# How the sample tokens' values reach all partitions: a DRAM buffer in place of selection matmuls

## The chip, the core and the metric

The kernel runs on one core of a Trainium2 chip. The metric is the device time in microseconds of one execution. Five engines run side by side, each with an instruction queue of its own that is worked off in order: TensorE (PE; its weight loads are shown apart as PEld), VectorE (DVE), ScalarE (ACT), GpSimd (POOL) and SyncE (SP). POOL and SP are used here mostly to issue DMAs; a DMA that must wait for something holds up what stands behind it on the queue of the engine that issues it.

## The reference, cut to what matters

The whole is one inference step of two decoder layers for 256 prompt tokens and 8 sample tokens (one token of each of 8 requests). Layer 0 attends over a window, layer 1 is a gated linear recurrence (HGRN2) with 12 heads, each with a state matrix of 128 x 128 for every request. The change concerns the recurrence for the 8 sample tokens:

```python
q, f, iv, mq, g = _split(jnp.einsum('btd,de->bte', h, w_in), HG_SPLITS)
fg = lb + (1.0 - lb) * jax.nn.sigmoid(f)
qh, kh, vh = jax.nn.silu(q), 1.0 - fg, iv
# one token: o and the new state
o = (q . k) v + (q * fg) @ state
state = fg[..., None] * state + k[:, None] * v[None, :]
```

(The last two lines write out what the chunked form of the reference comes to for one token.) The new state of every request and head is an output, 8 x 12 x 128 x 128 numbers in f32. All inputs and outputs are f32.

## The kernel before

**Layout.** Features lie on partitions, tokens along a row: 256 prompt and 8 sample tokens (T = 264). A product in near-f32 accuracy is made of f16 halves: each weight block of 128 x 2048 is loaded as f32 (`raw`), ScalarE writes the high half (line 92), VectorE the rest (line 93), and TensorE makes three passes (lines 297 to 299). One projection is 48 matmuls of 264 columns.

**The stream.** `Stream` walks over a list of units, each a weight block or a piece of cache or state with a function that uses it. Four `raw` buffers and four split buffers `hl` are in turn; loads are issued by SP (line 77) as buffers come free. A state block (one head's state, 8 requests x 128 x 128; added in lines 1154 to 1157) is split too, but its f32 form is held until its unit is done, since the new state is written into it and stored from it.

**Layer 1, per pair of heads.** Units run in the order f, f, v, v, q, state, (g), q, state, (g); g only for the first eight heads (four pairs). After each pair a side job `hg_side` does the recurrence of the prompt in pieces between the projections that follow. The order in which each engine takes its instructions is set when the program is built, by a scheduler that simulates the engines with assumed durations: what is written one after the other may be moved.

**The sample tokens' path.** `hv_unit` (line 930) projects v for one head and keeps it in f32 (`vt`) and, for the 8 sample columns, as f16 halves (`vs`). `hv_rows` (line 948) runs one unit later: it transposes the prompt part (line 952) and the halves (line 955, `hvr`), and VectorE copies the 16 rows to `vr` (line 956). `state_unit` (line 1106) then forms q times the forget gate (qf) and q times k (qk), multiplies the split state with qf (lines 1127, 1128: `hos`), sums qk over the partitions with an f32 matmul against constant weights (line 1130), and puts the output together (lines 1131 to 1133). For the new state every partition needs the row v of a request: a matmul with a selection matrix `sel` copies row b of `vr` to all 128 partitions in PSUM (line 1137, `vb`, four requests to a bank, eight matmuls a head). ScalarE scales the old state by the forget gate (line 1141), VectorE adds k times v (line 1142), and POOL stores the result (line 1145, `out_ss`).

**What stands near.** On POOL the store of the prompt's state (`out_sp`, line 1075). On VectorE the SiLU of q (line 728, `hqs`), on which the products `hd` (line 1030) and, over qa (line 1031) and qsp (line 987), the products `hs` on TensorE wait.

Of the kernel before, what the change touches and what calls it, by code (L numbers as in the profile page):

```python
# [32 lines left out]
SW = 1024.0  # L33
SA = 8.0
SP = 1024.0
SK = 2048.0
CP = 1.0 / (SW * SA)
# [92 lines left out]
def trunk_kernel(  # L130
# [17 lines left out]
    ident_d: bass.AP,  # L148
    onehot_d: bass.AP,
    mask_d: bass.AP,  # L150
    sel_d: bass.AP,
    y_o: bass.AP,
    mk_o: bass.AP,
    mv_o: bass.AP,
# [7 lines left out]
    nc = tc.nc  # L162
    mm = nc.tensor.matmul

    cp = ctx.enter_context(tc.tile_pool(name="cp", bufs=1))
# [3 lines left out]
    def bank(tag, bufs, name):  # L169
        return ps.tile([P, 512], F32, tag=tag, name=name, bufs=bufs)  # L170
# [21 lines left out]
    nc.gpsimd.memset(nones, -1.0 / P)  # L192
    ones_rms = cp.tile([P, P], F32, name="ones_rms")
    nc.vector.memset(ones_rms, 1.0 / 128.0)
    eps_rms = cp.tile([P, 1], F32, name="eps_rms")
    nc.vector.memset(eps_rms, RMS_EPS)

# [49 lines left out]
    def split_from(dst_hi, dst_lo, src, scale):  # L247
        split_all([(dst_hi, dst_lo, src)], scale)
# [631 lines left out]
    def open_l1():  # L880
        l0.close()
        p1 = l1.enter_context(tc.tile_pool(name="p1", bufs=1))
        H["p"] = p1
        H["mask"] = p1.tile([P, NMASK], I32, name="mask_t")
        nc.gpsimd.dma_start(H["mask"], mask_d)
        H["sel"] = p1.tile([2 * TS, TS, P], F16, name="sel_t")
        nc.gpsimd.dma_start(H["sel"], sel_d)
        H["ksp"] = [p1.tile([P, 2, 2, TP], F16, name=f"ksp{i}") for i in range(4)]
        for t in H["ksp"]:
            nc.gpsimd.memset(t, 0.0)  # L890

    def f_unit(h):
        def fn(hl):
            if h == 0:
                drain()
                open_l1()
            p1 = H["p"]
            pt = proj(hl, xhl, T, f"f{h}")
            i = h % 2
            if i == 0:  # L900
                cur["fg"] = p1.tile([P, 2, T], F32, tag="fg", name=f"fg{h}", bufs=2)
                cur["kk"] = p1.tile([P, 2, T], F32, tag="kk", name=f"kk{h}", bufs=2)
                cur["ks8"] = p1.tile([P, 2, TS], F32, tag="ks8", name=f"ks8{h}", bufs=2)
            fg, kk, ks8 = cur["fg"][:, i], cur["kk"][:, i], cur["ks8"][:, i]
            th = p1.tile([P, T], F32, tag="th", name=f"th{h}", bufs=2)
            nc.scalar.activation(th, pt, AF.Tanh, scale=0.5 * CP)
            half, mid, half_k, nhalf_k = (hl_lb[:, k, h : h + 1] for k in range(4))
            nc.scalar.activation(fg, th, AF.Identity, bias=mid, scale=half)
            nc.scalar.activation(kk, th, AF.Identity, bias=half_k, scale=nhalf_k)
            nc.vector.tensor_scalar_mul(ks8, kk[:, TP:T], 1.0 / (SA * SK))  # L910

        return fn

# [11 lines left out]

        return fn

    later, due = [], []

    def hv_unit(h):  # L930
        def fn(hl):
            p1 = H["p"]
            i = h % 2
            pt = proj(hl, xhl, T, f"hv{h}")
            if i == 0:
                cur["vn"] = p1.tile([P, 2, 2, P], F32, tag="vn", name=f"vn{h}", bufs=2)
                cur["vr"] = p1.tile([2 * TS, 2, P], F16, tag="vr", name=f"vr{h}", bufs=2)
                cur["vt"] = p1.tile([P, 2, T], F32, tag="vt", name=f"hvt{h}", bufs=1)
            vt = cur["vt"][:, i]
            vs = p1.tile([P, 2 * TS], F16, tag="vs", name=f"vs{h}", bufs=2)  # L940
            nc.scalar.activation(vt, pt, AF.Copy, scale=CP)
            split_from(vs[:, :TS], vs[:, TS:], pt[:, TP:T], 1.0 / SW)
            vn, vr = cur["vn"], cur["vr"]
            later.append(lambda: hv_rows(h, vt, vs, vn, vr))

        return fn

    def hv_rows(h, vt, vs, vn, vr):
        i = h % 2
        pt = bank("pt", 2, f"hvp{h}")  # L950
        for c in range(2):
            nc.tensor.transpose(pt[:, c * P : (c + 1) * P], vt[:, c * P : (c + 1) * P], ident)
        nc.scalar.activation(vn[:, i].rearrange("p c v -> p (c v)"), pt[:, :256], AF.Copy)
        p16 = ps.tile([2 * TS, P], F16, tag="pt", name=f"hvr{h}", bufs=2)
        nc.tensor.transpose(p16, vs, ident16)
        nc.vector.tensor_copy(vr[:, i], p16)

    def early_gate(j):
        def fn(hl):
# [146 lines left out]
    def state_unit(h):  # L1106
        def fn(hl):
            p1 = H["p"]
            pi, i = h // 2, h % 2
            raw = stream.raw[state_at[h]][:, : TS * P]  # L1110
            R = raw.rearrange("p (b v) -> p b v", b=TS)
            v = hl[:, :, : TS * P].rearrange("p s (b v) -> p s b v", b=TS)
            vr, fgs, ks8 = cur["vr"][:, i], cur["fg"][:, i, TP:T], cur["ks8"][:, i]
            qs, ks, vts = (cur[n][:, i, TP:T] for n in ("q", "kk", "vt"))
            if i == 0:
                osb[pi] = p1.tile([P, 2, T], F32, tag="osb", name=f"osb{pi}", bufs=2)
            qk = p1.tile([P, TS], F32, tag="qk", name=f"qk{h}", bufs=2)
            qf = p1.tile([P, TS], F32, tag="qf", name=f"qf{h}", bufs=2)
            qfh = p1.tile([P, TS, 2], F16, tag="qfh", name=f"qfh{h}", bufs=2)
            nc.vector.scalar_tensor_tensor(qf, qs, SA * 0.5 * CP, fgs, op0=ALU.mult, op1=ALU.mult)  # L1120
            nc.vector.scalar_tensor_tensor(qk, qs, P * 0.5 * CP / SK, ks, op0=ALU.mult, op1=ALU.mult)
            nc.scalar.activation(qfh[:, :, 0], qf, AF.Copy)
            nc.vector.tensor_tensor(qfh[:, :, 1], qf, qfh[:, :, 0], op=ALU.subtract)
            po = bank("ms", 1, f"hos{h}")
            pov = po[:, : 2 * TS].rearrange("p (b s) -> p b s", s=2)
            for b in range(TS):
                mm(pov[:, b], v[:, 0, b], qfh[:, b], start=True, stop=False)
                mm(pov[:, b, 0:1], v[:, 1, b], qfh[:, b, 0:1], start=False, stop=True)
            pq = po[:, 2 * TS : 3 * TS]
            mm(pq, ones_rms, qk, start=True, stop=True)  # L1130
            nc.vector.tensor_reduce(qf, pov, axis=AX.X, op=ALU.add)
            nc.vector.tensor_tensor(qk, pq, vts, op=ALU.mult)
            nc.vector.scalar_tensor_tensor(osb[pi][:, i, TP:T], qf, 1.0 / (SA * SA), qk, op0=ALU.mult, op1=ALU.add)
            for g in range(2):
                pvb = bank("pt", 2, f"vb{h}{g}")
                for bb in range(4):
                    mm(pvb[:, bb * P : (bb + 1) * P], H["sel"][:, 4 * g + bb], vr, start=True, stop=True)
# [77 lines left out]
def _constants():  # L1215
    c = {}
    c["ident"] = np.eye(P, dtype=np.float32)
    oh = np.zeros((33, 383 + P), np.float32)
    d = 255 - np.arange(383)
    ok = (d >= 0) & (d < 128)  # L1220
    oh[np.where(ok, _bucket(d), 32), np.arange(383)] = np.where(ok, 1.0 / CSWA, 1.0)
    slot = np.arange(P)
    oh[_bucket(np.where(slot == 0, 0, 128 - slot)), 383 + slot] = 1.0 / CSWA
    c["onehot"] = oh
    s = np.arange(P)
    m = np.zeros((P, NMASK), np.int32)
# [5 lines left out]
    sel = np.zeros((2 * TS, TS, P), np.float16)  # L1232
    for b in range(TS):
        sel[b, b] = 1
        sel[TS + b, b] = 1
    c["sel"] = sel
    return c


# [55 lines left out]
def unlayout(r):  # L1295
# [15 lines left out]

INS = [
    "xT", "memT", "w_kv", "w_in0", "w_in1", "w_mk", "w_mv", "w_o", "c_mk", "c_mv", "c_sk", "c_sv",
    "state", "small", "relb", "ident", "onehot", "mask", "sel",
]


# [18 lines left out]
```

## Time and profile before

| | |
|---|---|
| median of 3 runs | 912.54 us (911.29 to 913.2) |
| the profiled execution | 912.57 us, its span 910.8 us |
| mean granted TensorE clock | 0.995 |
| TensorE busy | 895.5 us (98%) |
| VectorE busy | 701.9 us (77%) |
| ScalarE busy | 577.0 us (63%) |
| moved by DMA | 198.41 MB, 218 GB/s over the span |

The span is the time from the first to the last instruction. A line such as "L1137 PE MATMUL vb<-vr,sel_t" names the line of the code, the engine, the operation, and the tile written and the tiles read. Start times are microseconds from the span's start. Matmuls overlap, so their durations add up to more than the time they take; what one costs is the distance from its start to the next one's. "<-" behind a waiting time names what ended it. A clock of 1.00 is full speed.

### The profile page before, as it was taken

How to read it: one execution, taken by the hardware profiler on the slowest of the kernel's cores; microseconds unless marked ns; L12 is line 12 of the kernel's file. 1: busy time of each engine (PE TensorE's matmuls, PEld its weight loads, DVE VectorE, ACT ScalarE, POOL GpSimd, SP SyncE). 2: the span in 40 equal slices, each digit the busy share in tenths (PEclk: the TensorE clock that was granted, in tenths of full speed). 3: DMA queues.
4: the chain of work that ended last, by engine and by line, in shares of the span. 5: the costliest groups of instructions: out<-in, count | busy, mean ns of one | idle time of the engine just before them, and what ended most of it. 6: DMA issues, size and time to landing. Idle time of an engine off the chain costs nothing.

```text
span 910.8 us, 21139 instructions
## 1 busy us (share of the span) xinstructions
PE 895.5 (98%) x8913; PEld 760.7 (84%) x8913; DVE 701.9 (77%) x1280; ACT 577.0 (63%) x980; POOL 34.6 (4%) x63
## 2 busy tenths in 40 slices
PE   9999999999999999999999999999999999899996
PEld 6888989678888888866888888888888888788885
DVE  6869877669886666696697897978789899767645
ACT  6757776567664543576766777676778676945323
POOL 1100010000000000002000000000000000000000
PEclk9999999999999999999999999999999999999998
DMA  9999566567685555555384555727454778566302
GB/s 345 383 335 330 189 244 217 194 210 259 257 320 189 204 208 187 191 203 195 127 308 146 196 183 185 282 100 268 150 212 165 264 270 318 186 226 230 141 1 96
DMA packets 36412, 198.41 MB, mean 218 GB/s; under 512 B 4572, under 2 KB 8445, under 8 KB 16093
## 3 DMA queue, kind: packets, MB, share of 16 engines
q1 hardware_dynamic: 31632, 181.55, 55.6%
q0 software_dynamic: 4640, 15.44, 4.6%
q8 instruction: 70, 1.15, 0.5%
q14 instruction: 26, 0.21, 0.1%
q10 hardware_dynamic: 44, 0.07, 0.0%
HBM read 179.80 MB, written 17.22 MB: 216 GB/s over the span
## 4 chain that ended last, share of the span: by engine, by line
PE 87%; ACT 5%; DVE 5%; DMA 2%; issue 1%; SPq 0%; ACTq 0%; DVEq 0%
PE o L297 6%; PE o L299 6%; PE o L298 6%; PE g L299 6%; PE g L297 6%; PE g L298 6%; PE q L297 2%; PE hv L298 2%; PE hv L297 2%; PE q L298 2%; PE q L299 2%; PE hv L299 2%; ACT hl L92 2%; PE f L299 2%; PE f L297 2%; PE f L298 2%
## 5 line engine op out<-in xcount | busy, mean ns | idle before, releaser
L93 DVE SCALAR_TENSOR_TENSOR hl<-raw,hl 128x2048 f16<-128x2048 f32 (+2 forms) x176 | 376.9, 2145 | 96.6 <-ACT hl L92 95.9
L92 ACT ACTIVATE hl<-raw 128x2048 f16<-128x2048 f32 (+2 forms) x176 | 314.2, 1790 | 118.1 <-PE o L299 73.9
L297 PEld LDWEIGHTS <-hl 128*128 128x128 f16 (+1 forms) x2176 | 209.9, 98 | 34.0 <-issue 2.9
L299 PEld LDWEIGHTS <-hl 128*128 128x128 f16 (+1 forms) x2176 | 209.9, 98 | 33.4 <-DVE hl L93 2.1
L298 PEld LDWEIGHTS <-hl 128*128 128x128 f16 (+1 forms) x2176 | 209.9, 98 | 32.1 <-issue 1.6
L299 PE MATMUL g<-xhl,hl 128*128 128x264 f16 x512 | 141.3, 276 | 1.5 <-DVE hl L93 1.5
L297 PE MATMUL g<-xhl,hl 128*128 128x264 f16 x512 | 141.5, 276 | 0.0
L298 PE MATMUL g<-xhl,hl 128*128 128x264 f16 x512 | 141.3, 276 | 0.0
L299 PE MATMUL o<-mix,hl 128*128 128x264 f16 x512 | 141.2, 276 | 0.0
L298 PE MATMUL o<-mix,hl 128*128 128x264 f16 x512 | 141.2, 276 | 0.0
L297 PE MATMUL o<-mix,hl 128*128 128x264 f16 x512 | 140.8, 276 | 0.3 <-DVE xres L742 0.3
L297 PE MATMUL q<-xhl,hl 128*128 128x264 f16 x192 | 53.0, 276 | 1.0 <-DVE kst L245 1.0
L297 PE MATMUL f<-xhl,hl 128*128 128x264 f16 x192 | 52.9, 276 | 0.4 <-DVE mvhl L245 0.4
L297 PE MATMUL hq<-xhl,hl 128*128 128x264 f16 x192 | 53.0, 276 | 0.0
L298 PE MATMUL hq<-xhl,hl 128*128 128x264 f16 x192 | 53.0, 276 | 0.0
L299 PE MATMUL hq<-xhl,hl 128*128 128x264 f16 x192 | 53.0, 276 | 0.0
L298 PE MATMUL hv<-xhl,hl 128*128 128x264 f16 x192 | 53.0, 276 | 0.0
L297 PE MATMUL hv<-xhl,hl 128*128 128x264 f16 x192 | 53.0, 276 | 0.0
L299 PE MATMUL hv<-xhl,hl 128*128 128x264 f16 x192 | 53.0, 276 | 0.0
L298 PE MATMUL q<-xhl,hl 128*128 128x264 f16 x192 | 53.0, 276 | 0.0
L299 PE MATMUL q<-xhl,hl 128*128 128x264 f16 x192 | 53.0, 276 | 0.0
L299 PE MATMUL f<-xhl,hl 128*128 128x264 f16 x192 | 52.9, 276 | 0.0
(311 smaller groups left out, 1625.4 us busy)
## 6 DMA issues: line engine op xcount, KB each, us to landing
raw<-in_w_in SPq DMA_DIRECT2D x88, 1024.0 KB, 5.8
raw<-in_w_o SPq DMA_DIRECT2D x32, 1024.0 KB, 4.9
raw<-in_w_mk SPq DMA_DIRECT2D x8, 1024.0 KB, 4.8
raw<-in_w_mv SPq DMA_DIRECT2D x8, 1024.0 KB, 5.1
raw<-in_c_mk SPq DMA_DIRECT2D x8, 1024.0 KB, 5.2
raw<-in_c_mv SPq DMA_DIRECT2D x8, 1024.0 KB, 4.9
raw<-in_state SPq DMA_DIRECT2D x12, 512.0 KB, 5.0
out_ss<-raw POOLq DMA_DIRECT2D x12, 512.0 KB, 2.9
```

What stands on the lines that cost most here:

```text
L92: hi = self.nc.scalar.activation(hl[:, 0, s], raw[:, s], AF.Copy, scale=scale)
L93: lo = self.nc.vector.scalar_tensor_tensor(hl[:, 1, s], raw[:, s], scale, hl[:, 0, s], op0=ALU.mult, op1=ALU.subtract)
L297: mm(out, lhs(0), rhs(0), start=start, stop=False)
L298: mm(out, lhs(0), rhs(1), start=False, stop=False)
L299: return mm(out, lhs(1), rhs(0), start=False, stop=stop)
```

## The change

The matrix `sel` and its matmuls go. `hv_rows` now transposes the last 128 columns of `vt` in f32, a third transpose beside the two for the prompt; the 8 sample rows come out on partitions 120 to 127. VectorE copies the upper 32 partitions to `vr`, a DMA stores the 8 rows (4 KB) in a DRAM tile `rows`, and a second DMA reads these 4 KB into every partition (`vb`, 128 x 4 KB = 512 KB; the source has a step of 0 over partitions). The f16 halves `vs` are no longer made. `state_unit` reads `vb` from SBUF. The sum over partitions of qk is made from two f16 halves (`qkh`) with f16 weights `ones16` instead of one f32 matmul.

```diff
+    ones16 = cp.tile([P, P], F16, name="ones16")
+    nc.vector.memset(ones16, 0.125)
...
-        H["sel"] = p1.tile([2 * TS, TS, P], F16, name="sel_t")
-        nc.gpsimd.dma_start(H["sel"], sel_d)
...
-            nc.vector.tensor_scalar_mul(ks8, kk[:, TP:T], 1.0 / (SA * SK))
+            nc.vector.tensor_scalar_mul(ks8, kk[:, TP:T], 1.0 / SK)
...
-            vs = p1.tile([P, 2 * TS], F16, tag="vs", name=f"vs{h}", bufs=2)
             nc.scalar.activation(vt, pt, AF.Copy, scale=CP)
-            split_from(vs[:, :TS], vs[:, TS:], pt[:, TP:T], 1.0 / SW)
...
         for c in range(2):
             nc.tensor.transpose(pt[:, c * P : (c + 1) * P], vt[:, c * P : (c + 1) * P], ident)
+        nc.tensor.transpose(pt[:, 256:384], vt[:, T - P : T], ident)
         nc.scalar.activation(vn[:, i].rearrange("p c v -> p (c v)"), pt[:, :256], AF.Copy)
-        p16 = ps.tile([2 * TS, P], F16, tag="pt", name=f"hvr{h}", bufs=2)
-        nc.tensor.transpose(p16, vs, ident16)
-        nc.vector.tensor_copy(vr[:, i], p16)
+        vr = p1.tile([P, P], F32, tag="vr", name=f"vr{h}", bufs=2)
+        nc.vector.tensor_copy(vr[96:P], pt[96:P, 256:384])
+        rows = dp.tile([TS, P], F32, name=f"rows{h}")[:, :]
+        nc.gpsimd.dma_start(rows, vr[P - TS : P])
+        every = bass.AP(tensor=rows.tensor, offset=rows.offset, ap=[[0, P], [1, TS * P]])
+        vb[h] = p1.tile([P, TS * P], F32, tag="vb", name=f"vb{h}", bufs=2)
+        nc.gpsimd.dma_start(vb[h], every)
...
-            nc.vector.scalar_tensor_tensor(qk, qs, P * 0.5 * CP / SK, ks, op0=ALU.mult, op1=ALU.mult)
+            nc.vector.scalar_tensor_tensor(qk, qs, 8.0 * 0.5 * CP / SK, ks, op0=ALU.mult, op1=ALU.mult)
+            qkh = p1.tile([P, 2, TS], F16, tag="qkh", name=f"qkh{h}", bufs=2)
+            nc.scalar.activation(qkh[:, 0], qk, AF.Copy)
+            nc.vector.tensor_tensor(qkh[:, 1], qk, qkh[:, 0], op=ALU.subtract)
...
-            mm(pq, ones_rms, qk, start=True, stop=True)
+            for s in range(2):
+                mm(pq, ones16, qkh[:, s], start=s == 0, stop=s == 1)
...
-            for g in range(2):
-                pvb = bank("pt", 2, f"vb{h}{g}")
-                for bb in range(4):
-                    mm(pvb[:, bb * P : (bb + 1) * P], H["sel"][:, 4 * g + bb], vr, start=True, stop=True)
-                for bb in range(4):
-                    b = 4 * g + bb
-                    s = R[:, b]
-                    nc.scalar.activation(s, s, AF.Copy, scale=fgs[:, b : b + 1])
-                    nc.vector.scalar_tensor_tensor(
-                        s, pvb[:, bb * P : (bb + 1) * P], ks8[:, b : b + 1], s, op0=ALU.mult, op1=ALU.add
-                    )
+            for b in range(TS):
+                s = R[:, b]
+                nc.scalar.activation(s, s, AF.Copy, scale=fgs[:, b : b + 1])
+                nc.vector.scalar_tensor_tensor(
+                    s, vb[h][:, b * P : (b + 1) * P], ks8[:, b : b + 1], s, op0=ALU.mult, op1=ALU.add
+                )
```

The scheduler puts the instructions in a new order. Two places follow, both at heads 4 and 5; a number behind a name tells one buffer's use from another's, and "waits" names what a row waits for (DMASW and DMAHW are DMAs issued by POOL and by SP).

VectorE before, from the end of head 4's output (qf, qk, osb) over its updates (raw_7031) to the splits behind them (hl_7624 is g of head 5, hl_7694 the first f of the next pair):

```order
L1131 TENSOR_REDUCE qf_7552<-hos_7558 128x8 [waits PE_49]
L1132 TENSOR_TENSOR qk_7551<-hos_7558,hvt_7350 128x8
L1142 SCALAR_TENSOR_TENSOR raw_7031<-vb_7579,ks_7188,raw_7031 128x128 [waits DMASW5_49,PE_49]
L1142 SCALAR_TENSOR_TENSOR raw_7031<-vb_7579,ks_7188,raw_7031 128x128
L1133 SCALAR_TENSOR_TENSOR osb_7550<-qf_7552,qk_7551 128x8 [waits DVE_49]
L1142 SCALAR_TENSOR_TENSOR raw_7031<-vb_7579,ks_7188,raw_7031 128x128 x2
L1142 SCALAR_TENSOR_TENSOR raw_7031<-vb_7592,ks_7188,raw_7031 128x128 [waits PE_49]
L1142 SCALAR_TENSOR_TENSOR raw_7031<-vb_7592,ks_7188,raw_7031 128x128 x3
L93 SCALAR_TENSOR_TENSOR hl_7624<-raw_7606,hl_7624 128x2048 [waits DMAHW2_49,Activation_49]
L728 SCALAR_TENSOR_TENSOR mix<-mix,g_7627 128x264 [waits Activation_49]
L93 SCALAR_TENSOR_TENSOR hl_7694<-raw_7608,hl_7694 128x2048 [waits DMAHW3_49,PE_49,Activation_49]
```

VectorE now, from the split of g of head 5 (hl_7597) over the updates of head 4 (raw_7009) and of head 5 (raw_7210) to the SiLU of head 5's q (hqs):

```order
L93 SCALAR_TENSOR_TENSOR hl_7597<-raw_7579,hl_7597 128x2048 [waits DMAHW2_49,Activation_49]
L1000 TENSOR_TENSOR prod_7723<-prod_7723 128x16 [waits DVE_49]
L1143 SCALAR_TENSOR_TENSOR raw_7009<-vb_7447,ks_7166,raw_7009 128x128 [waits DMASW6_49,DMASW4_49]
L1143 SCALAR_TENSOR_TENSOR raw_7009<-vb_7447,ks_7166,raw_7009 128x128 x7
L729 SCALAR_TENSOR_TENSOR mix<-mix,g_7600 128x264 [waits Activation_49]
L1000 TENSOR_TENSOR prod_7723<-prod_7723 128x8 [waits DVE_49]
L93 SCALAR_TENSOR_TENSOR hl_7667<-raw_7581,hl_7667 128x2048 [waits DMAHW3_49,PE_49,Activation_49]
L1143 SCALAR_TENSOR_TENSOR raw_7210<-vb_7524,ks_7166,raw_7210 128x128 [waits DMASW1_49]
L1143 SCALAR_TENSOR_TENSOR raw_7210<-vb_7524,ks_7166,raw_7210 128x128 x7
L1002 SCALAR_TENSOR_TENSOR prod_7723<-prod_7723 128x4 [waits DVE_49]
L1100 SCALAR_TENSOR_TENSOR osq_7593<-osb_6733,small_t,osq_7593 128x264 [waits Activation_49]
L729 SCALAR_TENSOR_TENSOR hqs_7501<-hqs_7501,hq_7670 128x264 [waits Activation_49]
```

The eight updates of a head now wait for a DMA (DMASW) and no longer for TensorE; the split of g stands ahead of head 4's updates, and head 5's updates stand ahead of its hqs (before, they stood behind it).

POOL before, from the stores of head 2's and head 3's new states to those of heads 4 and 5:

```order
L1145 DMA out_ss<-raw_6224 128x1024 [waits DMAHW4_49,DMASW4_49,DVE_49]
L1145 DMA out_ss<-raw_6425 128x1024 [waits DMAHW7_49,DMASW5_49,DVE_49]
L1075 DMA out_sp<-s_7535 128x256 [waits DMASW6_49,DVE_49]
L1145 DMA out_ss<-raw_7031 128x1024 [waits DMAHW6_49,DMASW7_49,DVE_49]
L1145 DMA out_ss<-raw_7232 128x1024 [waits DMAHW1_49,DMASW0_49,DVE_49]
```

POOL now, the same stretch:

```order
L1146 DMA out_ss<-raw_6213 128x1024 [waits DMAHW4_49,DVE_49]
L1146 DMA out_ss<-raw_6414 128x1024 [waits DMAHW7_49,DMASW4_49,DVE_49]
L955 DMA rows_7445<-vr_7443 8x128 [waits DMASW5_49,DVE_49]
L958 DMA vb_7447<-rows_7445 128x1024 [waits DMASW7_49,DMASW5_49]
L1077 DMA out_sp<-s_7510 128x256 [waits DVE_49]
L955 DMA rows_7522<-vr_7520 8x128 [waits DMASW0_49,DVE_49]
L958 DMA vb_7524<-rows_7522 128x1024 [waits DMASW2_49,DMASW0_49]
L1146 DMA out_ss<-raw_7009 128x1024 [waits DMAHW6_49,DVE_49]
L1146 DMA out_ss<-raw_7210 128x1024 [waits DMAHW1_49,DMASW3_49,DVE_49]
```

Each head adds a store and a load, the load waiting for its store; out_sp, the other head's pair and the two out_ss stand behind them.

On TensorE the third transpose stands with the other two, and all three now come later: for head 4 in the projection of its g, 13 matmuls in, before in that of its q, 19 matmuls in. The second hd of head 5 stands 41 projection matmuls behind the end of its q (22 before), the first hs of the pair 90 (44 before).

More of the change, by code (lines that the diff above doesn't have):

```diff
@@ L150, in trunk_kernel @@
     mask_d: bass.AP,
-    sel_d: bass.AP,
     y_o: bass.AP,
@@ L926, in hq_unit @@
         return fn
-    later, due = [], []
+    later, due, vb = [], [], {}
     def hv_unit(h):
@@ L936, in fn, with hv_rows @@
                 cur["vn"] = p1.tile([P, 2, 2, P], F32, tag="vn", name=f"vn{h}", bufs=2)
-                cur["vr"] = p1.tile([2 * TS, 2, P], F16, tag="vr", name=f"vr{h}", bufs=2)
                 cur["vt"] = p1.tile([P, 2, T], F32, tag="vt", name=f"hvt{h}", bufs=1)
             vt = cur["vt"][:, i]
-            vs = p1.tile([P, 2 * TS], F16, tag="vs", name=f"vs{h}", bufs=2)
             nc.scalar.activation(vt, pt, AF.Copy, scale=CP)
-            split_from(vs[:, :TS], vs[:, TS:], pt[:, TP:T], 1.0 / SW)
-            vn, vr = cur["vn"], cur["vr"]
-            later.append(lambda: hv_rows(h, vt, vs, vn, vr))
-        return fn
-    def hv_rows(h, vt, vs, vn, vr):
+            vn = cur["vn"]
+            later.append(lambda: hv_rows(h, vt, vn))
+        return fn
+    def hv_rows(h, vt, vn):
+        p1 = H["p"]
         i = h % 2
@@ L1112, in fn @@
             v = hl[:, :, : TS * P].rearrange("p s (b v) -> p s b v", b=TS)
-            vr, fgs, ks8 = cur["vr"][:, i], cur["fg"][:, i, TP:T], cur["ks8"][:, i]
+            fgs, ks8 = cur["fg"][:, i, TP:T], cur["ks8"][:, i]
             qs, ks, vts = (cur[n][:, i, TP:T] for n in ("q", "kk", "vt"))
@@ L1231, in _constants @@
     c["mask"] = m
[L1232 to L1236, printed above, removed]
     return c
@@ L1313 @@
     "xT", "memT", "w_kv", "w_in0", "w_in1", "w_mk", "w_mv", "w_o", "c_mk", "c_mv", "c_sk", "c_sv",
-    "state", "small", "relb", "ident", "onehot", "mask", "sel",
+    "state", "small", "relb", "ident", "onehot", "mask",
 ]
```

## The prediction

> **What bounds the kernel now.** I read the page first, then the table by stage, then TensorE's waits inside the stage of the change, and last the chain of waits there. The page gives the busy shares, and further down the shares of the chain that ended last:
>
> ```profile
> PE 895.5 (98%) x8913; PEld 760.7 (84%) x8913; DVE 701.9 (77%) x1280; ACT 577.0 (63%) x980; POOL 34.6 (4%) x63
> ...
> PE 87%; ACT 5%; DVE 5%; DMA 2%; issue 1%; SPq 0%; ACTq 0%; DVEq 0%
> ```
>
> All twelve heads' sample work lies between 420 and 728 us. The table by stage has, for it and for the stage behind it: length, busy us and (in brackets) instructions of PE, PEld, DVE, ACT and POOL, granted clock, DMA share, GB/s:
>
> ```profile
> core 0 of [0], span 910.8 us
> 420.00:728.00 308.00, 307.22 (x3171) 266.79 (x3171) 251.11 (x543) 218.17 (x402) 14.31 (x24) 1.00 0.55 199
> 728.00:820.00 92.00, 88.85 (x1027) 77.52 (x1026) 77.59 (x127) 64.49 (x97) 0.55 (x1) 0.98 0.69 250
> ```
>
> TensorE is busy 307.22 of 308 us at full clock; VectorE 251.11 (82%), ScalarE 218.17 (71%). Inside that stage TensorE's largest wait is this one, 0.5 us in three pieces:
>
> ```profile
> PE hs L297 <- ACT qsp L987: 0.5, 3, 0.2
> ```
>
> So TensorE is the bound, and an instruction taken off it is time off the span, as long as the other engines still feed it. How close they are is seen in the chain of waits, which leaves TensorE three times, once in each of three pairs of heads (the first step off TensorE, start and length):
>
> ```profile
> 508.21 0.39 ACT mix L727
> ...
> 562.16 0.39 ACT mix L727
> ...
> 616.12 0.39 ACT mix L727
> ```
>
> and comes back to it, for heads 4 and 5, here:
>
> ```profile
> 579.43 0.19 PE hs L297
> ```
>
> For 17.3 us (562.16 to 579.43) ScalarE and VectorE work without a break, and TensorE, busy with projections all that time, arrives at the product hs just after them. There the two sides are level.
>
> **The change, part by part.** All sums are made against the profiled execution, 912.57 us, of which 910.8 are the span; the median of the runs is 912.54, so nothing is lost between the two.
>
> *Selection matmuls and the f32 sum, removed.* What an instruction costs on TensorE is the distance between starts, not its duration, since matmuls overlap. Head 4, then half a group of head 0, from TensorE's timeline (start, length, operation):
>
> ```profile
> 558.60 0.16 PE L1128 MATMUL hos<-qfh,hl 128*128 128x1 f16 x1
> 558.63 0.37 PE L1130 MATMUL hos<-qk,ones_rms 128*128 128x8 f32 x2
> 558.93 0.61 PE L1137 MATMUL vb<-vr,sel_t 16*128 16x128 f16 x8
> 559.47 0.29 PE L299 MATMUL g<-xhl,hl 128*128 128x264 f16 x1
> ```
>
> ```profile
> 450.57 0.28 PE L297 MATMUL g<-xhl,hl 128*128 128x264 f16 x1
> 450.78 0.39 PE L1137 MATMUL vb<-vr,sel_t 16*128 16x128 f16 x4
> 451.11 0.29 PE L298 MATMUL g<-xhl,hl 128*128 128x264 f16 x1
> ```
>
> From the last hos (558.60, itself 0.03) to the next projection (559.47) lie 0.84 us: the f32 sum and eight selection matmuls. Where the eight stand in two fours, each four costs 451.11 - 450.57 - 0.11 (the step of one projection matmul, 551.55 to 551.66 below) = 0.43 us, 0.10 of it ahead of its first matmul. The sum alone is the 0.30 us from its start to the first selection matmul less that 0.10, so a head with two fours costs 2 x 0.43 + 0.20 = 1.06 us. Eight heads have them together, four apart: 8 x 0.84 + 4 x 1.06 = 11.0 us. The new sum is two f16 matmuls of 8 columns; the nearest row is the hos just above, one every 0.03 us, so 12 x 0.06 = 0.7 us comes back. Net 10.3 us.
>
> *The transpose of the split rows (hvr), replaced by a third f32 transpose.* Two places, a hvr between projections and a pair of f32 transposes:
>
> ```profile
> 551.55 0.28 PE L299 MATMUL hq<-xhl,hl 128*128 128x264 f16 x1
> 551.66 0.28 PE L297 MATMUL hq<-xhl,hl 128*128 128x264 f16 x1
> 551.87 0.22 PE L955 MATMUL hvr<-ident,vs 128*16 128x128 f16 x1
> 552.02 0.29 PE L298 MATMUL hq<-xhl,hl 128*128 128x264 f16 x1
> ```
>
> ```profile
> 548.85 0.38 PE L952 MATMUL hvp<-ident,hvt 128*128 128x128 f32 x2
> 549.07 0.28 PE L298 MATMUL hq<-xhl,hl 128*128 128x264 f16 x1
> ```
>
> One hvr costs 552.02 - 551.66 - 0.11 = 0.25 us; one f32 transpose 0.22 / 2 = 0.11. Twelve heads: 12 x 0.14 = 1.7 us. TensorE thus loses 12.0 us, 2.0 per pair of heads. If all of it is time, 912.57 - 12.0 = 900.6 us.
>
> *VectorE and ScalarE.* The two halves of vs go, the two halves of qkh come, at the same size (8 columns). The copy of vr grows from 16 to 32 partitions and from f16 to f32. I take zero for these (an estimate: what each partition reads and writes hardly changes), on engines that are idle for a fifth of the stage and more. The 96 updates of the state now read vb from SBUF instead of PSUM. The trace has no such instruction; the nearest are two of one shape, the first with both operands in SBUF, the second with one in PSUM:
>
> ```profile
> L742 DVE SCALAR_TENSOR_TENSOR xres<-xres,o 128x264 f32<-128x264 f32 x32 | 13.6, 429 | 35.6 <-PE o L299 35.6
> ...
> L722 DVE SCALAR_TENSOR_TENSOR sil<-sil,mix 128x264 f32<-128x264 f32 x24 | 10.3, 431 | 2.4 <-ACT mix L628 2.0
> ```
>
> (The second row is the one with both in SBUF.) 429 against 431 ns: no difference, so zero. The table sel_t (one load), the memset of ones16 at the start (VectorE, while TensorE waits for its first weights) and the new constants cost nothing.
>
> *The two DMAs, added.* Per head a store of 4 KB to DRAM and a load of 512 KB from it, one waiting for the other, both on POOL's queue. The kernel has no such pair. The nearest rows are small and 512 KB transfers (median us to landing, then min/median/max for the vsn rows and for out_ss; out_sp from the window of this pair):
>
> ```profile
> raw<-in_state SPq DMA_DIRECT2D x12, 512.0 KB, 5.0
> out_ss<-raw POOLq DMA_DIRECT2D x12, 512.0 KB, 2.9
> raw<-vsn POOLq DMA_DIRECT2D x8, 1.0 KB, 4.4
> ```
>
> ```profile
> out_sp<-s POOLq DMA_DIRECT2D x1, 128.0 KB, 2.0
> ```
>
> ```profile
> DMA to landing us min/median/max: 1.6/4.4/5.4
> ```
>
> ```profile
> DMA to landing us min/median/max: 2.9/2.9/6.2
> ```
>
> Low end of the round trip 1.6 + 2.9 = 4.5 us, high end 5.4 + 6.2 = 11.6. I take 5.5, a little above 2.0 + 2.9, because out_sp and out_ss use the same queue at the same place (556 and 562 us), where few loads are in flight. The Trainium skill ("DMA: Bandwidth & Descriptors", Anatomy of one DMA) gives 2.0 us plus bytes/436e3, so 2.0 + 3.2 = 5.2 us; it adds that most of the fixed part is the confirmation of the write, slowest where the target is HBM, which speaks against sending rows through DRAM. The trace agrees in size: 2.0 and 2.9 us for what it would put at 2.3 and 3.2. With 5.2 or 5.5 the sum is the same.
>
> Who waits for the trip? VectorE, at the first of the eight updates of a head, and its queue is in order. By the new order, between the copy of vr4 and the first update of head 4 stand the two s, the chain of prod, one full split hl and small ones; from VectorE's timeline (two s, four prod, hl):
>
> ```profile
> 555.30 0.60 DVE L1074 SCALAR_TENSOR_TENSOR s<-s,prod,pu 128x128 f32<-128x128 f32 x2
> 555.94 0.43 DVE L998 TENSOR_TENSOR prod<-fg 128x256 f32<-128x256 f32 x1
> 556.40 0.99 DVE L998 TENSOR_TENSOR prod<-prod 128x128 f32<-128x128 f32 x4
> ...
> 561.50 2.29 DVE L93 SCALAR_TENSOR_TENSOR hl<-raw,hl 128x2048 f16<-128x2048 f32 x1
> ```
>
> These are 4.3 us, and the second copy, a predicated copy and five operations of 8 columns bring about 1.2 more (an estimate): 5.5 us, just the trip I expect. Behind the updates wait the next split hl and, after head 5's updates, hqs, for which the second hd on TensorE waits. That hd stands 41 projection matmuls behind hq in the new order and 22 before, 19 x 0.11 = 2.1 us further back, so TensorE begins to wait only when the trip passes 5.5 + 2.1 = 7.6 us. On POOL, vb4 waits for rows4 to land, and out_sp, rows5, vb5 and out_ss of head 4 queue behind it; out_ss frees the buffer for which the weight loads on SP wait. I price that at zero: head 5's updates now stand ahead of hqs, so its out_ss leaves earlier, and four splits are held ahead of TensorE.
>
> *What is late next.* In the level stretch (562 to 579 us, and its like in two other pairs) VectorE and ScalarE set the pace. The selection matmuls of the odd head and its f32 sum lie in it, about 0.85 us a pair (0.64 and 0.20), 2.5 in all. In an unchanged order this would return as a wait. The new order puts the first hs of that pair 46 projection matmuls later (90 instead of 44 behind hq), which speaks for none of it returning; but other places may come level in its stead, so I charge half, 1.2 us: 900.6 + 1.2 = 901.8.
>
> **The rivals.**
>
> *VectorE's and ScalarE's chain takes over (906.6 us).* With 12 us off TensorE, VectorE is at 251 / 296 = 85%, and there are more level places than the one the chain shows. For it: the 17 us stretch, and hs waits that are already there. Against it: only 0.5 us of waits in 308, and four splits of reserve. Price: half the saving, 912.57 - 6.
>
> *The round trip holds VectorE up (slower).* Mechanism: VectorE stands at the first update, the split and hqs behind it come late, TensorE stands at hd. It decides from 7.6 us of trip; each us more costs 6 pairs x 1 us; at 7.6 + 12.0/6 = 9.6 us the gain is gone; at the high end 11.6 it is 900.6 + 6 x 4.0 = 924.6 us. For it: vsn's median 4.4 plus in_state's 5.0 make 9.4, both with loads of 1 MB in flight, and the share of DMA time in this stage is 0.55. Against it: the 2.0 and 2.9 at the very place. The Trainium skill ("TensorE: Matmul & The Clock Gate", Part 1) says that an idle window of some 3.4 us halves the clock; the granted clock of 1.00 in this stage has no such gap to show it, and by that rule this rival would lie some 10 us higher still.
>
> *Nothing left (912.5 us).* The same mechanism at a trip of about 9.6 us, or a worse order in the stage from 728 to 820 us, where TensorE already idles 3.2 us.
>
> **How the numbers follow.** Forecast 901.8 us (900 to 903.5): 0.50. The chain takes over, 903.5 to 910: 0.27. Slower through the round trip: 0.10. Nothing left: 0.08. Better than 900, because the orders around the heads close up as well: 0.05. Faster is 0.50 + 0.27 + 0.05 = 0.82; 0.2% (1.8 us) is about what a measurement of this kernel can tell from no change, so same is 0.08 and slower 0.10. The range runs from 899.5 to 911: it leaves out the slower case, most of the unchanged one and the tail below, some 0.2.
>
> **What would show it.** Right: TensorE's busy time between 420 and the end of the heads smaller by about 12 us and its waits there under 2 us; rows landing in about 2 us, vb in about 3; VectorE's wait for vb under 1 us a head; the update still 345 ns. The chain rival shows as TensorE waiting for qsp, kk or hl with no DMA behind it; the slow one as VectorE idle at the update with vb as releaser and hd waiting for hqs. I am wrong if vb takes over 6 us to land, if the update gets longer from SBUF, or if waits move to stages that the change doesn't touch.

## The result: slower, and the profile after

The changed kernel takes 924.38 us (median of 4 runs, 921.34 to 928.0) beside 912.87 us before; the ratio is 1.0122, with a 95% interval of 1.0093 to 1.0151. I had forecast 901.8. The profiled execution took 928.0 us, its span 926.2, so it is the longest of the four. Two executions further down, 1853.12 us in unread_1exp and 1029.61 us in gated_1exp, were disturbed, and the medians of these two runs leave them out.

The page of the changed kernel, busy time of the engines:

```profile
PE 890.3 (96%) x8817; PEld 757.5 (82%) x8817; DVE 702.4 (76%) x1281; ACT 586.3 (63%) x986; POOL 46.7 (5%) x86
```

The table by stage of the changed kernel, same columns and stretches as in the prediction:

```profile
420.00:728.00 308.00, 291.88 (x3021) 255.59 (x3019) 244.25 (x526) 217.69 (x397) 24.24 (x44) 0.99 0.60 213
728.00:820.00 92.00, 83.20 (x941) 71.51 (x940) 76.98 (x131) 66.25 (x96) 1.62 (x3) 0.91 0.68 247
```

TensorE is busy 15.3 us less between 420 and 728 us, about what "would show it right" asked for, and yet the kernel is slower: busy time also falls when an engine waits. Two further readings are in these lines. ScalarE's total rose by 9.3 us (577.0 to 586.3), which no term of my sum had. And the granted clock behind the heads fell from 0.98 to 0.91.

TensorE's waits of the changed kernel from 420 to 820 us (total, times, longest), where before there was half a microsecond in the stage of the heads:

```profile
PE msc L298 <- ACT osq L1095: 4.3, 1, 4.3
PE mq L300 <- DVE hl L93: 4.1, 1, 4.1
PE hd L1032 <- ACT osq L1095: 4.1, 2, 2.1
PE hd L1032 <- DVE hqs L729: 3.5, 3, 1.6
PE f L298 <- DVE mix L729: 3.4, 3, 1.3
```

VectorE's two largest waits between 420 and 760 us, the usual one for ScalarE's half of a split, and a new one:

```profile
DVE hl L93 <- ACT hl L92: 28.2, 23, 6.4
DVE raw L1143 <- DMA vb<-rows: 19.7, 8, 3.8
```

The second is the wait of the slower rival, 19.7 us in eight of the twelve heads. Head 5 in detail, first VectorE (copy of vr, updates, SiLU of q), then POOL's DMA issues:

```profile
558.51 0.30 DVE L953 COPY vr<-hvp 32x128 f32<-32x128 f32 x1
...
570.50 2.19 DVE L1143 SCALAR_TENSOR_TENSOR raw<-vb,ks,raw 128x128 f32<-128x128 f32 x8 [3.35 <-DMA vb<-rows]
...
573.09 0.42 DVE L729 SCALAR_TENSOR_TENSOR hqs<-hqs,hq 128x264 f32<-128x264 f32 x1
```

```profile
559.23 0.51 POOL L955 DMA_DIRECT2D rows<-vr  x1
562.06 0.55 POOL L958 DMA_DIRECT2D vb<-rows  x1 [2.32 <-DMA rows<-vr]
```

From the end of the copy (558.81) to the first update lie 11.7 us: 0.4 to the issue of rows, 2.8 until vb is issued, 0.55 for that issue, 7.9 until it has landed (8.4 from the start of its issue, which is how the landing times are counted). A weight load that SP issued 0.3 us later was on its way for just as long:

```profile
raw<-in_w_in SPq DMA_DIRECT2D x1, 1024.0 KB, 8.3
vb<-rows POOLq DMA_DIRECT2D x1, 512.0 KB, 8.4
```

In this head the store (2.5 us) is near what I took (2.0); the load is not. Over all heads the store took 1.5 to 7.1 us, median 2.5, and the load 3.8 to 9.7, median 4.8:

```profile
DMA to landing us min/median/max: 3.8/4.8/9.7
```

Most of ScalarE's extra 9.3 us is seen in the groups by form: loads of activation tables, 1283 ns each, for the norm of the heads before

```profile
L1093 ACT ACT_TABLE_LOAD x6 | 7.7, 1283 | 0.1
L1095 ACT ACT_TABLE_LOAD x6 | 7.7, 1283 | 0.1
```

and now (L1095 is the Ln of the norm, L1097 its Exp, L728 the tanh of the SiLU, L609 an Exp of the memory's softmax):

```profile
L1095 ACT ACT_TABLE_LOAD x9 | 11.5, 1283 | 0.2
L1097 ACT ACT_TABLE_LOAD x6 | 7.7, 1283 | 0.1
L748 ACT ACT_TABLE_LOAD x2 | 2.6, 1283 | 0.0
L728 ACT ACT_TABLE_LOAD x2 | 2.6, 1283 | 0.0
...
L609 ACT ACT_TABLE_LOAD x1 | 1.3, 1283 | 0.0
```

The whole kernel has 22 table loads in place of 16, 7.7 us more. Before, ScalarE did Ln, Ln, Exp, Exp for the two heads of a pair, with two loads. In the new order it changes its table between the heads, at two pairs and once more behind the heads, ahead of msc. ScalarE of the changed kernel in the stretch that I had called level:

```profile
566.70 1.28 ACT L1097 ACT_TABLE_LOAD   x1
568.00 0.42 ACT L1097 ACTIVATE osq<-osq 128x264 f32<-128x264 f32 x1
568.44 1.28 ACT L1095 ACT_TABLE_LOAD   x1
569.73 0.48 ACT L1095 ACTIVATE osq<-rms,eps_rms 128x264 f32<-128x264 f32 x1
570.23 1.28 ACT L728 ACT_TABLE_LOAD   x1
571.52 0.39 ACT L728 ACTIVATE hqs<-hq 128x264 f32<-128x264 f32 x1
```

So two suspects stood side by side after the first look: the wait for vb, and the table loads.

### The profile page after: what moved, and what is told of

Read it like the earlier page. It is cut to its first block, busy times and chain, and to the rows that moved or that the text cites. A ratio compares the mean times of both kernels' runs of the same rounds, so it can differ in the third digit from the quotient of the medians.

```text
span 926.2 us, 21002 instructions
## 1 busy us (share of the span) xinstructions
PE 890.3 (96%) x8817; PEld 757.5 (82%) x8817; DVE 702.4 (76%) x1281; ACT 586.3 (63%) x986; POOL 46.7 (5%) x86
```

## The experiments

"Heads" below is the time from TensorE's first f projection of layer 1 to its first mq projection, "behind" from there to the first o projection, both from its timeline; "loads" counts table loads. These three columns come from the one profiled execution of each run and the time is the median of its runs: the profiled execution of the changed kernel is the longest of its four, those of after_1exp and last_unread_1exp the shortest of theirs. Ratios are against runs of the kernel before on the same chip.

| run | us | ratio (95%) | heads | behind | loads |
|---|---|---|---|---|---|
| before | 912.87 | | 289.2 | 95.3 | 16 |
| changed | 924.38 | 1.0122 (1.0093 to 1.0151) | 291.1 | 110.3 | 22 |
| no_trip | 912.31 | 0.9984 (0.9968 to 0.9999) | 285.9 | 95.6 | 22 |
| unread | 913.07 | 0.9991 (0.9977 to 1.0005) | 285.9 | 95.9 | 22 |
| rows_now | 931.37 | 1.0206 (1.018 to 1.0232) | 300.4 | 101.6 | 16 |
| sum16 | 925.55 | 1.0135 (1.0114 to 1.0156) | 290.1 | 106.0 | 20 |
| after_1exp | 921.83 | 1.0109 (1.0073 to 1.0144) | 286.1 | 103.8 | 16 |
| no_trip_1exp | 901.74 | 0.9882 (0.9863 to 0.9901) | 276.8 | 96.2 | 16 |
| before_1exp | 915.08 | 1.0021 (1.0008 to 1.0034) | 290.1 | 95.7 | 16 |
| sum16_1exp | 919.7 | 1.0073 (1.0052 to 1.0094) | 290.1 | 100.1 | 16 |
| unread_1exp | 901.66 | 0.987 (0.9853 to 0.9887) | 276.8 | 96.0 | 16 |
| gated_1exp | 922.94 | 1.0104 (1.0087 to 1.0121) | 283.3 | 107.6 | 16 |
| small_vb_1exp | 920.96 | 1.0081 (1.0065 to 1.0098) | 293.5 | 99.9 | 16 |
| last_unread_1exp | 920.15 | 1.0075 (1.0053 to 1.0098) | 286.9 | 102.9 | 16 |
| first_unread_1exp | 906.83 | 0.9932 (0.9906 to 0.9957) | 276.9 | 101.3 | 16 |
| hybrid_1exp | 911.13 | 0.9973 (0.9959 to 0.9988) | 287.5 | 99.9 | 16 |

**The wait or the traffic: no_trip and unread.** One leaves the DMAs out, the other issues them and reads an old tile.

```diff
-                    s, vb[h][:, b * P : (b + 1) * P], ks8[:, b : b + 1], s, op0=ALU.mult, op1=ALU.add
+                    s, xres[:, b, :P], ks8[:, b : b + 1], s, op0=ALU.mult, op1=ALU.add
```

> The changed kernel without its two DMAs per head; the updates of the state read an old tile (xres) in place of vb, so the sample values are left out of the new state. Theory A (VectorE's wait for the round trip is what costs): the saving of TensorE comes through, 900 to 903 us, no wait at the updates, clock of 0.99 and more from 728 to 820 us. Rival B (the chain of VectorE and ScalarE or the new order takes the saving, the trip adds little): 908 us or more, with TensorE waiting for hqs, mix or qsp as in the changed kernel. Rival C (the transfers cost by crowding the DMA engines and POOL's queue): 900 to 903, like A.

> The changed kernel with both DMAs as they are, but the updates read an old tile (xres), so nothing waits for vb; the sample values are left out of the new state. Theory A (the wait costs): within 2 us of the run without the DMAs, 900 to 905. Rival B (chain or order): 908 or more, like the run without the DMAs. Rival C (the transfers crowd the weight loads or hold up out_ss on POOL): 912 or more, TensorE waiting for splits whose loads came late.

912.31 and 913.07 us. The two agree within their intervals, so the traffic and POOL's queue cost nothing that can be measured: rival C falls, though 913.07 lies in its band. Without the wait 12 us come back, but theory A asked for 900 to 903: it falls as the only cause. Both numbers lie in rival B's band, and its sign is there too: in both, TensorE waits three times for 2.2 us (unread; hd for the SiLU of q), once in each of the three pairs of heads 2 to 7:

```profile
PE hd L1032 <- DVE hqs L729: 6.5, 3, 2.2
```

and ahead of it, on ScalarE of no_trip, four table loads in a row, where the kernel before has two (L1090 Ln, L1092 Exp):

```profile
562.18 1.28 ACT L1090 ACT_TABLE_LOAD   x1
563.48 0.48 ACT L1090 ACTIVATE osq<-rms,eps_rms 128x264 f32<-128x264 f32 x1
563.98 1.28 ACT L1092 ACT_TABLE_LOAD   x1
565.27 0.42 ACT L1092 ACTIVATE osq<-osq 128x264 f32<-128x264 f32 x1
565.71 1.28 ACT L1090 ACT_TABLE_LOAD   x1
...
567.50 1.28 ACT L1092 ACT_TABLE_LOAD   x1
...
570.80 0.37 ACT L728 ACTIVATE hqs<-hq 128x264 f32<-128x264 f32 x1
```

Two loads more are 2.57 us, and hd waits 2.2. The second theory: the table loads cost as much as the wait, each where the other leaves room.

**The transposes and DMAs written earlier: rows_now.**

```diff
-            later.append(lambda: hv_rows(h, vt, vn))
+            hv_rows(h, vt, vn)
```

> The changed kernel with the transposes of v, the copy of vr and both DMAs written directly behind the projection of v, not one unit later; the whole computation is done. Theory A: the copy of vr comes some 10 us or more sooner against the updates, so vb is there when VectorE comes: waits for vb under 3 us in all (19.7 in the changed kernel), 901 to 906 us. Rival B: 910 or more though VectorE no longer waits for vb. Rival C: the transfers are as many as before, so 915 or more.

931.37 us. The number lies in rival C's band, but C had fallen with unread, and what A and B both expected, no wait at vb, did not come: the wait grew to 30.4 us, in all twelve heads.

```profile
DVE raw L1143 <- DMA vb<-rows: 30.4, 12, 5.3
```

The copy of vr was to come 10 us sooner; counted from the first f projection it came 4.0 us sooner at most, 2.2 for head 4 and not at all for head 5. And in the new order the eight updates have moved forward: those of head 4 now stand ahead of the SiLU of its own q and of osb, where they stood behind the split of g. VectorE waits 2.1 us for them, and 2.4 for those of head 5, 11.2 us behind the copy. So writing the trip earlier in the source didn't shorten the wait: the scheduler moved both ends of it.

**The f16 sum alone: sum16.** Before, with only this part of the change:

```diff
-            mm(pq, ones_rms, qk, start=True, stop=True)
+            for s in range(2):
+                mm(pq, ones16, qkh[:, s], start=s == 0, stop=s == 1)
```

> The kernel before with only the f16 sum of qk (two f16 matmuls and the two halves of qk in place of one f32 matmul); selection matmuls stay. By the prediction's terms: 12 x (0.20 - 0.06) = 1.7 us less, 910.9 us, ratio 0.998. Rival B (the halves of qk cost as much on VectorE and ScalarE, or the order gets worse): no change or slower, 912.5 or more.

925.55 us, in rival B's band: slower by 1.35% for an edit that was to take 1.7 us off TensorE. By the distances between starts, summed over the heads, the sum itself went from 3.0 to 0.9 us, a little more than worked out. But in the new order the 96 selection matmuls stand in 27 groups and not in 16 (8.1 us and not 7.0, from the start of each group to the matmul behind it), and ScalarE has four table loads more, all behind the heads, where 10.7 us are lost.

**The table loads: the 1exp runs.** One Exp over both heads, so that it must stand behind both Ln:

```diff
+        both = p1.tile([P, 2, T], F32, tag="osq", name=f"osq{pi}", bufs=1)
+        sqs = [both[:, 0], both[:, 1]]
...
-        for i, sq in enumerate(sqs):
-            nc.scalar.activation(sq, sq, AF.Exp, scale=-0.5)
+        nc.scalar.activation(both, both, AF.Exp, scale=-0.5)
+        for i, sq in enumerate(sqs):
```

> The changed kernel with one Exp instruction over both heads of a pair in place of two, so that ScalarE can't do Ln, Exp, Ln, Exp (whole computation done; 16 table loads in its order, as in the kernel before; the changed kernel has 22). Theory A (two things cost: the six extra table loads of 1.28 us on ScalarE's chain, and VectorE's wait for vb): the loads go, the wait stays, 912 to 918 us. Rival B (the wait for vb alone is the cause): 921 or more. Rival C (the loads alone): 905 or less.

> The run without the DMAs (updates read an old tile, sample values left out of the new state), with one Exp instruction over both heads of a pair. Theory A: the three waits of 2.2 us of hd for hqs go with the six extra table loads, the 10 to 12 us taken off TensorE come through, 900 to 906 us. Rival D (VectorE and ScalarE are level with TensorE anyway, so the wait returns at another place): 909 or more with TensorE's waits in the stage of the heads still 6 us or more.

> The kernel before with one Exp instruction over both heads of a pair. Control: it had 16 table loads and has 16 now; by theory A no change beyond 0.3%, 911 to 914. Rival E (any edit that makes the scheduler write a new order costs some per cent, whatever the edit): 918 or more.

> The kernel before with the f16 sum, and one Exp instruction over both heads of a pair: 16 table loads, where the f16 sum alone has 20. Theory A (the four extra loads, at the last two pairs, and the clock that falls with the waits there are its 12 us): 910 to 914. Rival E (a new order costs, whatever the edit; the loads are not its cause): 918 or more.

> The changed kernel with one Exp instruction a pair (16 table loads), both DMAs as they are, but the updates read an old tile, so that nothing waits for vb (sample values left out of the new state). Theory A (what is left in the changed kernel with one Exp, 921.8 us, is the wait for vb, not the traffic): within 2 us of the same kernel without the DMAs (901.7), 900 to 904. Rival C (crowding or POOL's queue): 910 or more.

The control moves by 0.2% (915.08, a little outside what I expected, on the slow side), so the edit by itself gains nothing. Without the wait it is worth 10.6 us (912.31 to 901.74) or 11.4 (913.07 to 901.66): theory A holds, rival D falls. unread_1exp, with all the new transfers in flight but without the sample values in the new state, is at 901.66 us; this is the change with its two unforeseen costs taken out. That it lies 0.1 us from my forecast is in part luck: on its chip the kernel before took 913.72 us, so it saves 12.1, TensorE's whole 12.0, and the 1.2 us that I charged for the level stretch are not there. Its stage of the heads shows a TensorE that hardly waits:

```profile
420.00:728.00 308.00, 307.58 (x3246) 271.77 (x3244) 265.85 (x570) 226.88 (x413) 25.38 (x46) 1.00 0.64 235
```

With the wait left in (after_1exp) the same edit gives only 2.6 us, within the spread: 921.83, above the 912 to 918 that I expected and in the band of rival B (the wait alone). So the four corners are 924.4 (both costs), 921.8 (wait), 912.3 to 913.1 (loads), 901.7 (none). The wait costs 20 us alone and 12 beside the loads, the loads 11 alone and 3 at most beside the wait. Rival B falls by the other corner, where the loads cost 11 us without the wait. Both costs hold up the same hqs, and the later of the two sets it: in head 5 of the changed kernel ScalarE is done with hqs at 571.9 us, VectorE comes to it at 573.1. One reservation: every run has an order of its own (six of the extra loads stand in the heads without the wait, four with it), so the corners show the size of each cost and not a sum to the last us. sum16_1exp (919.7, loads back at 16) lies in rival E's band and loses 4.6 us against before_1exp, 4.4 of it behind the heads; the loads were half of its loss, and the other half, in a kernel whose own sum got shorter, I put down to the order.

**Bytes or order: small_vb_1exp and gated_1exp.** The first loads one eighth; the second gives each update a factor that depends on a later SiLU, and writes the transposes and DMAs early.

```diff
-        every = bass.AP(tensor=rows.tensor, offset=rows.offset, ap=[[0, P], [1, TS * P]])
+        every = bass.AP(tensor=rows.tensor, offset=rows.offset, ap=[[0, P], [1, P]])
```

```diff
+                src = mix[:, h, :TS] if i == 0 and h < NG1 else cur["q"][:, 1, :TS]
+                nc.vector.scalar_tensor_tensor(gk, src, 0.0, ks8, op0=ALU.mult, op1=ALU.add)
```

> The changed kernel with one Exp instruction a pair, and a load vb of one eighth (128 columns, 64 KB, every update reads these; seven of eight values are left out). Theory A1 (the trip is long because the 512 KB share the DMA engines with weight loads of 1 MB): vb lands in 2 to 3 us in place of 4 to 9, VectorE's waits for it fall from 12 us to under 6, 905 to 915 us. Rival A2 (the trip is long by the fixed cost of two DMAs one after the other and POOL's queue): vb still 4 us or more, waits as before, 918 or more.

> The changed kernel with one Exp instruction a pair, the transposes and both DMAs written directly behind the projection of v, and the factor of the updates made to depend on a later tile (the SiLU of g or of q, times zero), so that the scheduler can't put the updates ahead of it; the whole computation is done. Theory A (the scheduler puts the updates where it believes vb to be there, and that is too soon): VectorE waits for vb under 3 us in all, the saving of TensorE comes through less a little for the state's buffer held longer, 901 to 907 us, faster than both kernels. Rival F (the buffer held longer stops the weight loads): 910 or more, TensorE waiting for hl with a late load behind it.

The load of 64 KB lands in 3.4 us (median) and not in 4.4, in 6.1 and not 8.0 at worst (after_1exp), and the time stays (920.96); VectorE waits 15.6 us for it (12.4 in after_1exp), and the first update stands 8.6 us (median) behind the copy of vr and not 9.6, as if the scheduler reckoned with the smaller load. Neither A1 nor A2 as I had put them: the trip did get shorter, and the wait did not. gated_1exp has no wait for vb left, and its heads take 283.3 us, 6.0 less than before: the reading of the wait holds. But 922.94 us in all, in rival F's band: it loses 12 us behind the heads. There TensorE waits 12.7 us, 4.7 of them for a split (hl), which with a late load behind it was F's sign, and most of the rest for the recurrence, the first two of these lines for that of the last pair (hs):

```profile
776.37 0.20 PE L301 MATMUL hs<-qsp,ksp 128*128 128x64 f16 x1 [2.06 <-ACT ksp L992]
778.72 0.24 PE L303 MATMUL hs<-qsp,ksp 128*128 128x64 f16 x1 [2.12 <-DVE ksp L993]
...
795.85 0.40 PE L303 MATMUL g<-xhl,hl 128*128 128x264 f16 x1 [2.89 <-DVE hl L94]
```

How much of this is F isn't shown: ScalarE waits 9.6 us there for weight loads that land late (2.3 in the kernel before), and what that passes on to the recurrence was not tested.

**Behind the heads: last_unread_1exp, first_unread_1exp, hybrid_1exp.** In the first only heads 10 and 11 read the old tile, in the second only heads 0 to 9; the hybrid is the gated kernel for heads 0 to 7 with the old selection matmuls for heads 8 to 11.

```diff
-                    s, vb[h][:, b * P : (b + 1) * P], ks8[:, b : b + 1], s, op0=ALU.mult, op1=ALU.add
+                    s, vb[h][:, b * P : (b + 1) * P] if h < 10 else xres[:, b, :P], ks8[:, b : b + 1], s, op0=ALU.mult, op1=ALU.add
```

> The changed kernel with one Exp instruction a pair, in which only the last two heads' updates read an old tile (their sample values left out), so only the last pair has no wait for vb. Theory G (the loss behind the heads is that pair's wait: its recurrence starts late, the projections of the memory queries and the gates run out, and the clock falls): from the first mq projection to the first o 96 us, as without the DMAs, in place of 103.7; about 8 us less, 912 to 915 us. Rival H (the loss there is lateness carried over from the pairs before, or the order): 919 or more.

> The counterpart: the changed kernel with one Exp instruction a pair, in which heads 0 to 9 read an old tile (their sample values left out) and only the last pair waits for its vb. Up to the last pair its order is that of the run in which nothing waits. Theory G (the last pair's wait, with what it moves, makes the loss behind the heads): 100 us or more from the first mq projection to the first o, 906 to 911 us in all. Rival H (the loss there comes from the pairs before, through the order that their waits give the last pair): 96 to 98 us there, 902 to 905 in all.

> The gated kernel (one Exp a pair, transposes and DMAs directly behind the projection of v, updates held behind the SiLU) for heads 0 to 7, and the selection matmuls of the kernel before for heads 8 to 11; the whole computation is done. Theory G: no vb is waited for in the last pairs, so the stages behind the heads take the 95 us of the kernel before and the first four pairs keep their gain: 904 to 909 us, faster than both kernels. Rival H (the stages behind the heads are late by the order whatever the last pairs do): 912 or more.

The last pair's wait alone costs 5 us behind the heads (101.3 beside 96.0, and 906.83 beside 901.66), though VectorE stands only 2.3 us at vb there. Taking it alone away gives nothing back (102.9 beside 103.8; rival H's 919 or more, 920.15): what the earlier pairs' waits leave to the last pair, its order or the lateness carried over, is then enough to lose as much. Each is shown to suffice; what does it in the second case stays open. The hybrid, a complete kernel, takes 911.13 us, 0.27% less than before, in no band that I gave, but below both kernels.

## Why the prediction was wrong, point by point

**TensorE's saving: right.** 12.0 us forecast; the heads of unread_1exp take 12.4 us less than before (276.8 beside 289.2).

**"The two DMAs, added": failed in size, and in what sets the wait.** I took 5.5 us for the trip and 5.5 until VectorE arrives. I worked it out for head 4, and there it was near: vb had landed 6.1 us behind the copy, VectorE came after 7.3 and did not wait. But it is head 5's updates that stand ahead of hqs, and its trip I did not price. The trip of heads 3, 5 and 7 was 11.1 to 12.1 us (head 11: 16.0; all twelve: 6.1 to 16.0, median 8.5), at my high end. In head 5 the load of 512 KB took 8.4 and not 2.9 us, with a weight load of 1 MB and out_ss on their way beside it; in head 9 it was the store (7.1 us). The load took over 6 us, which I had named as a sign of being wrong, in four heads of twelve. out_ss, from which I took 2.9, was no safe neighbour: it takes 6.9 us (median) itself between 440 and 760 us of the changed kernel. I also read VectorE's arrival from the order as if it were given. The runs show that it isn't: with the trip written earlier (rows_now) or the load made smaller (small_vb_1exp) the updates moved too and the wait stayed; only a dependency (gated_1exp) took it away. That the scheduler puts the updates where its own model has vb landed fits all three, but no run shows that model.

**"I take zero for these" on ScalarE: failed.** I compared sizes of instructions and looked at the new order of VectorE, POOL and TensorE, not at ScalarE's. Six more table loads of 1283 ns stood in it, four of them in the stretch where ScalarE and VectorE set the pace. Their price is 11 us where nothing waits for vb, and 3 at most beside the wait.

**"What is late next": failed.** I charged 1.2 us for the level stretch. Without loads and wait nothing came back there (unread_1exp: TensorE waits 0.4 us in the whole stage), but it had no slack for 2.57 us of loads or 3 us of waiting.

**"Nothing left ... a worse order in the stage from 728 to 820 us"** was a clause of a rival and turned out to be worth 15 us of profiled time (95.3 to 110.3).

**The slower rival named the right mechanism, and its 924.6 us agree with 924.4 by chance.** It priced 4 us a pair at hd. The heads lost 1.9 us net, in which TensorE's waits (12.0 us between the first f and the first mq) eat the saving; the rest of the loss is behind the heads. There the mechanism has a second price, the clock. TensorE of the changed kernel, after VectorE had come late from vb of head 10 to the split that mq needs:

```profile
710.19 0.28 PE L299 MATMUL mq<-xhl,hl 128*128 128x264 f16 x1
714.61 0.31 PE L300 MATMUL mq<-xhl,hl 128*128 128x264 f16 x1 [4.14 <-DVE hl L93]
714.73 0.41 PE L298 MATMUL mq<-xhl,hl 128*128 128x264 f16 x1
714.93 0.42 PE L299 MATMUL mq<-xhl,hl 128*128 128x264 f16 x1
```

and the granted clock around it, by microsecond:

```profile
713.00:714.00 1.00, 0.00 (x0) 0.00 (x0) 1.00 (x1) 0.00 (x0) 0.17 (x1) 1.00 0.27 111
714.00:715.00 1.00, 0.39 (x3) 0.31 (x4) 0.94 (x3) 0.00 (x0) 0.00 (x0) 0.87 0.99 410
715.00:716.00 1.00, 1.00 (x6) 0.67 (x5) 1.00 (x4) 0.00 (x0) 0.51 (x1) 0.50 0.50 86
```

After 4.14 us of idling the matmuls start 0.22 us apart and not 0.11, for 3.3 us (to 718.0). The Trainium skill ("TensorE: Matmul & The Clock Gate", Part 1) has this rule, an idle window of about 3.4 us and half the clock until one has been busy; this place agrees. Shorter waits can do the same in these runs: in no_trip TensorE waits 2.16 us (to 515.98) and then makes steps of 0.22 us until 519.9, while behind its waits of 2.15 us at 571.8 and 626.0 us the clock stays at 1.00. So a wait of 2.2 us can already bring half the clock in these runs, and need not. The clock of no_trip, third number from the end:

```profile
518.00:520.00 2.00, 2.00 (x12) 1.39 (x11) 2.00 (x5) 0.00 (x0) 0.00 (x0) 0.52 0.00 0
```

Summed over the windows behind the heads (busy time by one less the clock), the lower clock costs 8.3 us in the changed kernel and 1.5 before, with 12.9 and 2.9 us of idling. In the prediction I had put some 10 us for it behind the slower rival alone.

## What to carry to other kernels

An edit that makes a scheduler write a new order is priced by the new order of every engine, also of the one that the edit hardly touches: count what a change of order can add there (table loads, groups torn apart) before taking zero. Where the scheduler chooses the place of the instruction that waits for a DMA, neither writing the DMA sooner nor making it smaller took the wait away here; a real dependency that holds the consumer back did, but it did not make the kernel faster. A trip has to be priced for every head that something waits for, not for the first of a pair alone. Two delays in the same place don't add, and removing one of them can show little: test them in pairs.

## What the runs showed that I had not expected

A small edit of one sum (sum16) made the kernel 1.35% slower through the order that it brought. In the norm of the heads a change from Ln to Exp cost a table load of 1283 ns each way, with the next activation 1.29 to 1.30 us after the load's start where it waited for nothing else. The Trainium skill ("ScalarE: Activation LUTs", Table sets: the hidden batching unit) says that one set has both Ln and Exp, so that an Exp behind a Ln needs no second load. In the layer norms this holds: there the kernel loads that set by name (`natural_log_exp_and_others`, line 748 of the changed kernel), and no load stands between the Ln (L778) and the Exp (L779):

```profile
380.84 0.42 ACT L778 ACTIVATE r<-rstd 128x264 f32<-128x264 f32 x1 [1.73 <-DVE rstd L776]
381.30 0.42 ACT L779 ACTIVATE r<-r 128x264 f32<-128x264 f32 x1
```

The norm of the heads names no set, and the built program puts a load ahead of each change there. Whether naming the set would take these loads away, no run shows. The 6 MB of broadcast loads cost nothing that can be measured by their traffic (901.66 beside 901.74 us), though they made the weight loads slower to land, 6.2 us median and not 5.2 between 420 and 740 us (unread_1exp beside no_trip_1exp).
